# A hybrid attention, RWKV-7 and PEER layer on one core: packed parameters, another order of the first loads, and other queues for three loads of the last stage

## The chip, the cores and the metric

The kernel runs on one NeuronCore of a Trainium2 chip. The metric is the device time of one execution in microseconds. The core has five engines with instruction streams of their own: TensorE (PE, with its weight loads as PEld), VectorE (DVE), ScalarE (ACT), GpSimd (POOL) and SyncE (SP, which here only issues transfers). Each engine takes its instructions in order, and an instruction that waits holds all that stand behind it on that engine. Transfers are issued by SP, ACT or POOL, each into a queue of its own, and are carried by 16 DMA engines that the three queues share.

## The reference, cut to what matters

```python
mod = silu(c) @ ada_w + ada_b                       # shift, scale, gate of two sub-layers
h   = rms_norm(x, norm1_g) * (1 + scale1) + shift1  # x is 1024 tokens x 1024
z   = h @ w_in
x   = x + gate1 * (concat(attention(z), rwkv7(z)) @ w_out)
h2  = rms_norm(x, norm2_g) * (1 + scale2) + shift2
x   = x + gate2 * peer_ffn(h2)

def peer_ffn(h):   # 16384 experts of one neuron each, 8 heads x 16 of them for each token
    # product keys choose the experts e_idx and their gates
    act = gelu(einsum('cd,ced->ce', h, expert_u[e_idx]))
    return einsum('ce,ced->cd', gate * act, expert_v[e_idx])
```

## The kernel before

The program is recorded step by step through a framework that allots buffers from pools, adds the waits that buffers and data ask for, and fixes one order for each engine. Where several lists of steps run side by side, `merge` and `due` in the source say which step comes at what point; the order that results is on record before the run.

**The front** (lines 105 to 266). Some small parameters (`c`, parts of `ada_b`, `norm1_g`, `mu_prev`, `mu_next`, the two norm gains) are loaded in transposed form, one element for each partition and column, by SP's and ACT's queues (L117 to L129); seven more of the same kind (`colp`, L319) come by POOL's. `tables` builds masks on VectorE. Then SP loads sixteen 512 KB tiles `adw` of `ada_w`, and VectorE adds them up in two accumulators `macc` (L223, L225); a first weight tile of `w_in` (two `wraw`) and eight tiles `xx` of x (512 KB each, L233) follow in SP's queue. ScalarE squares every `xx` into row sums (`jk`, L236), and the rows are scaled. Sixteen small products `mcol` turn `macc` into columns, and `h_step` writes the first operand of the input projection, `hTh` and `hTl` (L261 to L263). The first product that uses it is L314.

**The last stage** (from about 2260 us; lines 1750 to 1872) computes PEER in two ways at once. Three blocks of 128 tokens take their experts by gathers: POOL issues an indirect transfer of 512 KB for rows of `expert_u` (`gu`) or `expert_v` (`gv`) at L1361, and VectorE does the products (L1389, L1397). The other five blocks (640 tokens) go densely over all experts, in 128 tiles of 128 experts: for a tile n, `act_half` gives gelu(u h) as the tile `gl` (128 x 640), `gate` multiplies it on POOL with the gates `gt_` (L1771), ScalarE and VectorE split the product into `ah` and `al` (L1772, L1773), and TensorE multiplies these with the split expert rows `vh` and `vl` (L1791, L1792; products L1812 to L1814). VectorE adds the results to `yac` (L1821).

Of the 128 tiles 65 have their gelu computed early, before this stage, and stored in HBM (`actd`); `gate_load` brings such a tile back (320 KB, L1761). `g_load` brings the gates for four tiles (1.25 MB, L1765). `u_load` brings the 512 KB of a tile whose gelu is still to be computed (L1438), `v_load` brings 256 KB of expert rows (L1785). All four are issued by SP.

The stage runs in 32 groups of four tiles; in a group the stored tiles (two, in most groups) come first. Pools limit what can be ahead: two buffers for `gl` (`NGL`), two for `gt_`, two for `u` (`NU`), four for `vr`, four each for `gu` and `gv`. The loads of a group are put into the program by

```python
at(s0, g_load, g)
...
at(s0 + 3 + k - GD, gate_load, n)
at(s0 + 3 + k, gate, n)
```

Of the kernel before, what the change touches and what calls it, by code (L numbers as in the profile page):

```python
# [20 lines left out]
D = 1024  # L21
NB = 8
# [56 lines left out]
def body(tc, nc, I, out, dbg=None):  # L79
# [3 lines left out]
    with root:  # L83
# [30 lines left out]


        scol = ct([128, NK], "scol")
        nc.sync.dma_start(scol, I["c"][0].rearrange("(o p) -> p o", p=128))  # L117
        bcol = ct([128, 16], "bcol")
        nc.scalar.dma_start(bcol, ada_b[0:2048].rearrange("(j p) -> p j", p=128))
        g1col = ct([128, NK], "g1col")  # L120
        nc.scalar.dma_start(g1col, I["norm1_g"][0].rearrange("(j p) -> p j", p=128))
        mup = ct([128, 14], "mup")
        nc.scalar.dma_start(mup, I["mu_prev"][0].rearrange("(j p) -> p j", p=128))
        mun = ct([128, 14], "mun")
        nc.scalar.dma_start(mun, I["mu_next"][0].rearrange("(j p) -> p j", p=128))
        gqk = ct([128, 2], "gqk")
        for i, nm in enumerate(("q_norm_g", "k_norm_g")):
            for h in range(2):
                nc.scalar.dma_start(gqk[64 * h:64 * h + 64, i:i + 1], I[nm][0].rearrange("(p o) -> p o", o=1))  # L129
        nc.scalar.activation(scol, scol, AF.Silu)  # L130
        nc.vector.tensor_scalar(gqk[:, 0:1], gqk[:, 0:1], HD ** -0.5, None, op0=ALU.mult)
# [96 lines left out]
        xt = []  # L228
        ssq = small("ssq", [128, NB])
        rstd = small("rstd", [128, NB])  # L230
        for tb in range(NB):
            xx = slot("xx")
            nc.sync.dma_start(xx, x[tb * 128:(tb + 1) * 128, :])  # L233
            xt.append(xx)
            jk = slot("jk")
            nc.scalar.activation(jk, xx, AF.Square, accum_out=ssq[:, tb:tb + 1])  # L236
            if tb % 4 == 3:
                r_ = rstd[:, tb - 3:tb + 1]
                nc.vector.tensor_scalar(r_, ssq[:, tb - 3:tb + 1], 1.0 / D, 1e-6, op0=ALU.mult, op1=ALU.add)
                rsqrt(r_, r_, [128, 4], "r1")  # L240
                for b in range(tb - 3, tb + 1):
                    if b < 4:
                        nc.vector.tensor_scalar(xt[b], xt[b], rstd[:, b:b + 1], None, op0=ALU.mult)
                    else:
                        nc.scalar.activation(xt[b], xt[b], AF.Copy, scale=rstd[:, b:b + 1])
        mcol = bank("mcol", "po")
# [71 lines left out]

        def colp(name, ap, n):  # L319
            t_ = fc([128, n], name)  # L320
            nc.gpsimd.dma_start(t_, ap.rearrange("(j p) -> p j", p=128))
            return t_

        w0 = [colp(f"w0{d}", I["w_decay0"][0][d], 4) for d in range(2)]
        a0 = [colp(f"a0{d}", I["a_gate0"][0][d], 4) for d in range(2)]
        kkc = colp("kkc", I["k_k"][0], 4)
        kac = colp("kac", I["k_a"][0], 4)
        rkc = colp("rkc", I["r_k"][0].rearrange("h e -> (h e)"), 4)
        ka1 = fc([128, 4], "ka1")
# [1097 lines left out]

        uts, ats = {}, {}
        early = [n for n in range(NT) if (n + 1) * NEARLY // NT > n * NEARLY // NT]
# [397 lines left out]
        def finish_half(tb, hf, y_):  # L1827
# [73 lines left out]
```

## Time and profile before

| | |
|---|---|
| three runs | 3858.38, 3872.6, 3874.69 us; median 3872.6 |
| profiled execution | 3867.33 us, its span 3865.2 us |
| busy share of the span | PE 85%, PEld 75%, DVE 78%, ACT 34%, POOL 45% |
| mean granted TensorE clock | 0.932 of full speed |
| moved by DMA | 862.66 MB, mean 223 GB/s |
| first `hTh` (operand of the input projection) begun | 51.41 us |

The span runs from the first to the last instruction of one execution. A busy share is an average over stages with different limits. The idle time that a view puts beside an instruction stands before it, with the event that ended it. The granted clock is given as a share of 2.4 GHz; 0.5 is 1.2 GHz.

### The profile page before, as it was taken

What the parts mean: (1) busy time and instruction counts of PE and PEld (TensorE: products, weight loads), DVE (VectorE), ACT (ScalarE), POOL (GpSimd) and SP (SyncE); (2) the same over time, 40 slices, a digit from 0 to 9 for tenths busy, and PEclk for the clock granted to TensorE, in tenths of its full rate; (3) what the DMA queues carried; (4) which work ended last, traced back from release to release, by engine and by line L of the source; (5) the groups of instructions that cost most, each with busy time, mean ns of one, the idle gap of its engine ahead of it and who ended that gap; (6) DMA issues with size and microseconds to landing.
All of it is one profiled execution on the core that took longest, in us unless ns stands there. A gap on an engine that the chain in (4) does not pass through costs nothing. (4 is left out here: it accounts for less than half of the span.)

```text
span 3865.2 us, 59635 instructions
## 1 busy us (share of the span) xinstructions
PE 3298.5 (85%) x21937; PEld 2906.7 (75%) x21937; DVE 3004.1 (78%) x5970; ACT 1317.4 (34%) x2710; POOL 1754.6 (45%) x1346
## 2 busy tenths in 40 slices
PE   4968899899697988878878878888889889899998
PEld 4747887677586987877777877777777777777787
DVE  6785556767747799999998977777777878778776
ACT  3234334455212322222377873222222222222221
POOL 2032211222334455466754527555555565655541
PEclk9988999999798988999998999999999999999999
DMA  6434444433464357566798988777777877777774
GB/s 200 177 124 138 140 102 111 113 95 82 124 203 176 115 164 238 173 211 214 270 329 275 342 286 330 285 284 285 289 289 290 301 289 290 291 289 290 295 271 160
DMA packets 493451, 862.66 MB, mean 223 GB/s; under 512 B 149348, under 2 KB 290404, under 8 KB 489064
## 3 DMA queue, kind: packets, MB, share of 16 engines
q1 hardware_dynamic: 372840, 447.20, 35.6%
q0 software_dynamic: 113280, 411.63, 29.0%
q8 instruction: 173, 2.83, 0.3%
q10 hardware_dynamic: 7040, 0.03, 0.1%
q14 instruction: 118, 0.97, 0.1%
HBM read 741.91 MB, written 116.80 MB: 222 GB/s over the span
## 5 line engine op out<-in xcount | busy, mean ns | idle before, releaser
L316 PE MATMUL pact<-dTh,uTl 128*128 128x320 f32 x2048 | 646.2, 317 | 53.9 <-DVE uTl L1449 53.7
L314 PE MATMUL pact<-dTh,uTh 128*128 128x320 f32 x2048 | 648.4, 317 | 24.6 <-ACT uTh L1448 14.3
L315 PE MATMUL pact<-dTl,uTh 128*128 128x320 f32 x2048 | 644.1, 315 | 0.0
L1361 POOL DMA_INDIRECT gu<-in_peer_u_dram,ei x384 | 532.2, 1386 | 221.9 <-DVE gu L1389 135.2
L1389 DVE SCALAR_TENSOR_TENSOR gu<-gu,ghr 128x1024 f32<-128x1024 f32 x384 | 510.1, 1329 | 154.9 <-DMA gu<-in_peer_u_dram,ei 148.3
L1812 PE MATMUL py<-vh,ah 128*128 128x512 f32 x1280 | 522.1, 408 | 98.8 <-DVE yac L1821 58.2
L1813 PE MATMUL py<-vl,ah 128*128 128x512 f32 x1280 | 525.2, 410 | 65.4 <-DVE vl L1792 65.0
L1361 POOL DMA_INDIRECT gv<-in_peer_v_dram,ei x384 | 499.2, 1300 | 158.5 <-issue 89.0
L1397 DVE SCALAR_TENSOR_TENSOR gacc<-gv,gact,gacc 128x1024 f32<-128x1024 f32 x381 | 526.5, 1382 | 54.1 <-DMA gv<-in_peer_v_dram,ei 51.1
L1814 PE MATMUL py<-vh,al 128*128 128x512 f32 x1280 | 517.8, 405 | 2.8 <-DVE al L1773 2.8
L316 PEld LDWEIGHTS pact<-dTh,uTl 128*128 128x128 f32 x2048 | 393.7, 193 | 61.2 <-DVE uTl L1449 61.2
L314 PEld LDWEIGHTS pact<-dTh,uTh 128*128 128x128 f32 x2048 | 395.0, 193 | 30.7 <-ACT uTh L1448 15.8
L315 PEld LDWEIGHTS pact<-dTl,uTh 128*128 128x128 f32 x2048 | 394.1, 192 | 2.5
L1812 PEld LDWEIGHTS py<-vh,ah 128*128 128x128 f32 x1280 | 252.3, 197 | 160.3 <-ACT gl L1460 37.5
L1813 PEld LDWEIGHTS py<-vl,ah 128*128 128x128 f32 x1280 | 252.4, 197 | 139.7 <-DVE vl L1792 88.9
L1814 PEld LDWEIGHTS py<-vh,al 128*128 128x128 f32 x1280 | 252.5, 197 | 56.7 <-DVE al L1773 3.3
L1791 ACT ACTIVATE vh<-vr 128x512 fp32r<-128x512 f32 x256 | 155.9, 625 | 395.8 <-PE py L1814 377.3
L1772 ACT ACTIVATE ah<-gl 128x640 fp32r<-128x640 f32 x128 | 91.2, 735 | 461.2 <-POOL gl L1771 323.5
L1705 DVE TENSOR_TENSOR o<-io,tT 128x1024 f32<-128x1024 f32 x160 | 187.0, 1217 | 34.2 <-ACT tT L161 24.8
L1718 PE MATMUL pgb<-o,o 128*128 128x128 f32 x1280 | 178.4, 295 | 39.0 <-ACT o L1708 29.6
L1448 ACT ACTIVATE uTh<-u 128x1024 fp32r<-128x1024 f32 x128 | 135.1, 1056 | 215.6 <-PE pact L315 174.3
L1773 DVE TENSOR_TENSOR al<-gl,ah 128x640 fp32r<-128x640 f32 x128 | 104.0, 832 | 132.7 <-ACT ah L1772 132.5
(1438 smaller groups left out, 7130.2 us busy)
## 6 DMA issues: line engine op xcount, KB each, us to landing
u<-in_peer_ut_dram SPq DMA_DIRECT2D x128, 512.0 KB
vr<-in_peer_v_dram SPq DMA_DIRECT2D x256, 256.0 KB
Gd<-st SPq DMA_DIRECT2D x160, 256.0 KB
actd<-gl SPq DMA_DIRECT2D x65, 320.0 KB
gl<-actd SPq DMA_DIRECT2D x65, 320.0 KB
awt<-in_ada_w_dram SPq DMA_DIRECT2D x32, 512.0 KB
wraw<-in_peer_w_query_dram SPq DMA_DIRECT2D x32, 512.0 KB
wraw<-in_w_in_dram SPq DMA_DIRECT2D x26, 512.0 KB
```

The costliest lines, as they stand in the source:

```text
L314: nc.tensor.matmul(ps, lh, rh, start=(i == 0), stop=False)
L315: nc.tensor.matmul(ps, lh, rl, start=False, stop=False)
L316: nc.tensor.matmul(ps, ll, rh, start=False, stop=(i == n - 1))
L1361: g_ = nc.gpsimd.indirect_dma_start(out=r_, out_offset=None, in_=src, in_offset=bass.IndirectOffsetOnAxis(ap=eid[tb][:, j:j + 1], axis=0))
L1389: nc.vector.scalar_tensor_tensor(u, u, 1.0, hr, op0=ALU.mult, op1=ALU.mult, accum_out=act[:, q:q + 1])
L1397: nc.vector.scalar_tensor_tensor(acc, v, pact[:, q:q + 1], acc, op0=ALU.mult, op1=ALU.add)
L1705: nc.vector.tensor_tensor(o_, io128[:, None, :].to_broadcast([128, 8, 128]), tT[:, i, t0:t0 + 8, None].to_broadcast([128, 8, 128]), ALU.is ...
L1718: nc.tensor.matmul(pg[:, q * 128:(q + 1) * 128], o1[:, 4 * x_ + q], o2[:, 4 * x_ + q], start=True, stop=True)
L1791: nc.scalar.activation(vh, vts[i], AF.Copy)
L1812: nc.tensor.matmul(ys[hf][b], ah[:, ts], vh, start=(n == tiles[0]), stop=False)
L1813: nc.tensor.matmul(ys[hf][b], ah[:, ts], vl, start=False, stop=False)
L1814: nc.tensor.matmul(ys[hf][b], al[:, ts], vh, start=False, stop=(n == tiles[-1]))
```

## The change

The small parameters are packed on the host side of the program into one array of 128 rows with 90 columns, which one transfer of SP loads; the fourteen small transfers of ACT's and POOL's queues, and that of `c`, are gone. The first four tiles of x are loaded, squared and scaled ahead of `ada_w`; the other four stay where they were. `ada_w` is loaded and added up half by half (all eight tiles of `macc[0]`, then those of `macc[1]`) and no longer alternately. In the last stage the stored tiles `gl` and the gates `gt_` are loaded by POOL's queue, and the `u` tiles by ACT's.

```diff
+        pk = ct([128, 90], "pk")
+        nc.sync.dma_start(pk, I["pk"])
...
+        ccol, bcol, g1col, mup, mun, gqk_ = (cols(n) for n in (NK, 16, NK, 14, 14, 2))
+        w0, a0 = [cols(4) for _ in range(2)], [cols(4) for _ in range(2)]
+        kkc, kac, rkc = (cols(4) for _ in range(3))
         scol = ct([128, NK], "scol")
-        nc.sync.dma_start(scol, I["c"][0].rearrange("(o p) -> p o", p=128))
-        bcol = ct([128, 16], "bcol")
-        nc.scalar.dma_start(bcol, ada_b[0:2048].rearrange("(j p) -> p j", p=128))
...
-        nc.scalar.activation(scol, scol, AF.Silu)
+        nc.scalar.activation(scol, ccol, AF.Silu)
+        nc.vector.tensor_copy(gqk, gqk_)
...
+        def x_in(tbs):
+            for tb in tbs:
+                xx = slot("xx")
+                nc.sync.dma_start(xx, x[tb * 128:(tb + 1) * 128, :])
...
+        x_in(range(4))
 
         macc = [slot("macc") for _ in range(2)]
-        for k in range(NK):
-            for i in range(2):
+        for i in range(2):
+            for k in range(NK):
...
+        x_in(range(4, NB))
...
-            nc.sync.dma_start(u, Ut[n])
+            (nc.scalar if late[0] else nc.sync).dma_start(u, Ut[n])
...
-                nc.sync.dma_start(ats[n], actd[early.index(n)])
+                nc.gpsimd.dma_start(ats[n], actd[early.index(n)])
...
-            nc.sync.dma_start(gts[q], Gd[q])
+            nc.gpsimd.dma_start(gts[q], Gd[q])
...
+        late[0] = True
```

Three places show what moves. On SP in the front, before (the loads of `ada_w`, the first weights, x):

```order
L1088 DMA gu<-in_g_up_dram 128x128
L221 DMA adw<-in_ada_w_dram 128x1024 x16
L180 DMA wraw<-in_w_in_dram 128x4x256 x2
L233 DMA xx<-in_x_dram 128x1024 x8
L180 DMA wraw<-in_w_in_dram 128x4x256 x2
```

and now:

```order
L1083 DMA gu<-in_g_up_dram 128x128
L223 DMA xx<-in_x_dram 128x1024 x4
L243 DMA adw<-in_ada_w_dram 128x1024 x16
L181 DMA wraw<-in_w_in_dram 128x4x256 x2
L223 DMA xx<-in_x_dram 128x1024 x4
L181 DMA wraw<-in_w_in_dram 128x4x256 x2
```

Four of the eight x tiles have moved ahead of the sixteen `adw`.

On POOL in the last stage, between two groups, before (`gu` and `gv` are gathers; `gl_31084` is the first stored tile of the new group, `gl_30959` the last tile of the group before):

```order
L1361 DMA gu_31038<-in_peer_u_dram,ei2_11948 128x1024
L1361 DMA gv_31040<-in_peer_v_dram,ei2_11948 128x1024
L1771 TENSOR_TENSOR gl_31084<-gl_31084,gt__31055 128x640
L1771 TENSOR_TENSOR gl_30959<-gl_30959,gt__30672 128x640
L1361 DMA gu_31078<-in_peer_u_dram,ei2_11948 128x1024
```

and the same place now, up to the load of the group's second stored tile, `gl_31089`:

```order
L1356 DMA gu_31014<-in_peer_u_dram,ei2_11924 128x1024
L1356 DMA gv_31016<-in_peer_v_dram,ei2_11924 128x1024
L1756 DMA gl_31060<-actd_11940 128x640
L1766 TENSOR_TENSOR gl_31060<-gl_31060,gt__31031 128x640
L1766 TENSOR_TENSOR gl_30935<-gl_30935,gt__30648 128x640
L1356 DMA gu_31054<-in_peer_u_dram,ei2_11924 128x1024
L1356 DMA gv_31056<-in_peer_v_dram,ei2_11924 128x1024
L1356 DMA gu_31083<-in_peer_u_dram,ei2_11924 128x1024
L1356 DMA gv_31085<-in_peer_v_dram,ei2_11924 128x1024
L1756 DMA gl_31089<-actd_11940 128x640
```

The load of a group's first stored tile stands right before the product that needs it, with no gather between; that of the second has four gathers between it and its use. In six of the later groups the load of `gt_` stands right before the first one too.

On ACT in the last stage a row of `u` now stands among the conversions (`uTh` and `vh` are the high parts of u and v, `gl` the gelu, `ah` the high part of the gated tile):

```order
L1443 ACTIVATE uTh_32560<-u_32376 128x1024
L1455 ACTIVATE gl_32286<-pact_32313 128x320
L1767 ACTIVATE ah_32409<-gl_32286 128x640
L1786 ACTIVATE vh_32443<-vr_32344 128x512
L1433 DMA u_32756<-in_peer_ut_dram 128x1024
L1786 ACTIVATE vh_32533<-vr_32382 128x512
```

Before, the same stretch of ACT has no transfer in it. The new tile takes the buffer of `u_32376`, which VectorE reads last (`uTl`, the low part).

## Rows read from the trace of the kernel before

**Rows 1.** Stretch of the last stage: length, busy us by engine, clock, DMA share, GB/s

```profile
2260.00:3865.00 1605.00, 1417.96 (x7046) 1221.26 (x7044) 1243.41 (x1600) 387.52 (x685) 869.38 (x643) 0.96 0.77 282
```

**Rows 2.** Waits from 2300 us on: who, for whom, us in total, times, longest

```profile
POOL gl L1771 <- DMA gl<-actd: 249.8, 21, 18.1
...
PE py L1813 <- DVE vl L1792: 65.0, 46, 5.2
PE py L1812 <- DVE yac L1821: 58.2, 21, 4.5
...
DVE gu L1389 <- DMA gu<-in_peer_u_dram,ei: 143.8, 51, 5.4
DVE al L1773 <- ACT ah L1772: 132.5, 31, 11.9
...
SPq L1438 <- DVE uTl L1449: 138.9, 29, 8.0
```

**Rows 3.** Timeline of POOL over three groups: start, us, instruction, idle time before it

```profile
3312.38 1.88 POOL L1771 TENSOR_TENSOR gl<-gl,gt__30286 128x640 f32<-128x640 f32 x1 [14.42 <-issue]
...
3346.59 1.03 POOL L1361 DMA_INDIRECT gv<-in_peer_v_dram,ei  x1 [0.30 <-issue]
3360.14 2.24 POOL L1771 TENSOR_TENSOR gl<-gl,gt__30672 128x640 f32<-128x640 f32 x1 [12.53 <-DMA gl<-actd]
...
3365.14 0.98 POOL L1361 DMA_INDIRECT gu<-in_peer_u_dram,ei  x1
...
3391.56 0.95 POOL L1361 DMA_INDIRECT gv<-in_peer_v_dram,ei  x1 [0.30 <-issue]
...
3410.65 1.57 POOL L1771 TENSOR_TENSOR gl<-gl,gt__31055 128x640 f32<-128x640 f32 x1 [18.14 <-DMA gl<-actd]
```

**Rows 4.** Timeline of SP's queue in the first of these waits

```profile
3346.82 9.20 SPq L1785 DMA_DIRECT2D vr<-in_peer_v_dram  x3
3356.12 0.38 SPq L1761 DMA_DIRECT2D gl<-actd  x1
```

**Rows 5.** The chain of work that ended last, in the same stretch: start, us, what

```profile
3356.12 3.87 DMA gl<-actd
...
3366.43 8.62 DMA gv<-in_peer_v_dram,ei
```

**Rows 6.** Timeline of VectorE in the same stretch

```profile
3345.38 0.81 DVE L1773 TENSOR_TENSOR al<-gl,ah 128x640 fp32r<-128x640 f32 x1
...
3354.99 0.68 DVE L1792 TENSOR_TENSOR vl<-vr,vh 128x512 fp32r<-128x512 f32 x1
...
3373.12 1.23 DVE L1389 SCALAR_TENSOR_TENSOR gu<-gu,ghr 128x1024 f32<-128x1024 f32 x1 [5.16 <-DMA gu<-in_peer_u_dram,ei]
...
3393.87 0.81 DVE L1773 TENSOR_TENSOR al<-gl,ah 128x640 fp32r<-128x640 f32 x1
```

**Rows 7.** Stretches of 4 us while POOL waits, columns as in rows 1

```profile
3348.00:3352.00 4.00, 4.00 (x14) 3.15 (x13) 4.00 (x5) 0.04 (x1) 0.00 (x0) 0.65 1.03 417
3352.00:3356.00 4.00, 4.00 (x29) 4.00 (x28) 4.00 (x8) 1.03 (x2) 0.00 (x0) 1.00 0.54 209
```

**Rows 8.** A plain transfer that POOL issues, line L1309: ns min, median, max

```profile
L1309 POOL DMA_DIRECT2D x1d<-x x8: 534/534/605, 1194.2 to 1209.3; - x8
```

**Rows 9.** Stretches of the front, columns as in rows 1

```profile
0.00:10.00 10.00, 0.00 (x0) 0.00 (x0) 0.21 (x4) 0.00 (x0) 7.39 (x18) 1.00 0.78 60
...
20.00:30.00 10.00, 0.00 (x0) 0.00 (x0) 10.00 (x11) 0.00 (x0) 0.00 (x0) 1.00 1.02 406
```

**Rows 10.** Timeline of the front: VectorE's first waits and sums, the first `hTh`

```profile
13.32 0.17 DVE L332 TENSOR_TENSOR mu<-mup,mun 128x14 f32<-128x14 f32 x1 [12.22 <-DMA mun<-in_mu_next_dram]
...
21.26 9.65 DVE L225 SCALAR_TENSOR_TENSOR macc<-adw,scol,macc 128x1024 f32<-128x1024 f32 x8
...
40.56 1.06 ACT L236 ACTIVATE jk<-xx 128x1024 f32<-128x1024 f32 x1 [0.42 <-DMA xx<-in_x_dram]
...
51.41 0.78 ACT L261 ACTIVATE hTh<-pt,sb,sg 128x512 fp32r<-128x512 f32 x1 [0.19 <-PE pt L257]
```

More of the change, by code (lines that the diff above doesn't have):

```diff
@@ L113, in body, with cols @@
         w_in = I["w_in"][0]
-        scol = ct([128, NK], "scol")
-        nc.sync.dma_start(scol, I["c"][0].rearrange("(o p) -> p o", p=128))
-        bcol = ct([128, 16], "bcol")
-        nc.scalar.dma_start(bcol, ada_b[0:2048].rearrange("(j p) -> p j", p=128))
[L120 to L125, printed above, removed]
+        pk = ct([128, 90], "pk")
+        nc.sync.dma_start(pk, I["pk"])
+        po_ = [0]
+        def cols(n):
+            po_[0] += n
+            return pk[:, po_[0] - n:po_[0]]
+        ccol, bcol, g1col, mup, mun, gqk_ = (cols(n) for n in (NK, 16, NK, 14, 14, 2))
+        w0, a0 = [cols(4) for _ in range(2)], [cols(4) for _ in range(2)]
+        kkc, kac, rkc = (cols(4) for _ in range(3))
+        scol = ct([128, NK], "scol")
         gqk = ct([128, 2], "gqk")
-        for i, nm in enumerate(("q_norm_g", "k_norm_g")):
-            for h in range(2):
-                nc.scalar.dma_start(gqk[64 * h:64 * h + 64, i:i + 1], I[nm][0].rearrange("(p o) -> p o", o=1))
-        nc.scalar.activation(scol, scol, AF.Silu)
+        nc.scalar.activation(scol, ccol, AF.Silu)
+        nc.vector.tensor_copy(gqk, gqk_)
         nc.vector.tensor_scalar(gqk[:, 0:1], gqk[:, 0:1], HD ** -0.5, None, op0=ALU.mult)
@@ L215, in body @@
         tables()
+        xt = []
+        ssq = small("ssq", [128, NB])
+        rstd = small("rstd", [128, NB])
+        def x_in(tbs):
+            for tb in tbs:
+                xx = slot("xx")
+                nc.sync.dma_start(xx, x[tb * 128:(tb + 1) * 128, :])
+                xt.append(xx)
+                jk = slot("jk")
+                nc.scalar.activation(jk, xx, AF.Square, accum_out=ssq[:, tb:tb + 1])
+                if tb % 4 == 3:
+                    r_ = rstd[:, tb - 3:tb + 1]
+                    nc.vector.tensor_scalar(r_, ssq[:, tb - 3:tb + 1], 1.0 / D, 1e-6, op0=ALU.mult, op1=ALU.add)
+                    rsqrt(r_, r_, [128, 4], "r1")
+                    for b in range(tb - 3, tb + 1):
+                        if b < 4:
+                            nc.vector.tensor_scalar(xt[b], xt[b], rstd[:, b:b + 1], None, op0=ALU.mult)
+                        else:
+                            nc.scalar.activation(xt[b], xt[b], AF.Copy, scale=rstd[:, b:b + 1])
+        x_in(range(4))
         macc = [slot("macc") for _ in range(2)]
-        for k in range(NK):
-            for i in range(2):
+        for i in range(2):
+            for k in range(NK):
                 a = slot("adw")
@@ L227, in body @@
         WT = {GO[0]: load_w(w_in, GO[0] * 256, nc.gpsimd)}
[L228 to L245, printed above, removed]
+        x_in(range(4, NB))
         mcol = bank("mcol", "po")
@@ L316, in mm3 @@
                 nc.tensor.matmul(ps, ll, rh, start=False, stop=(i == n - 1))
[L319 to L328, printed above, removed]
         ka1 = fc([128, 4], "ka1")
@@ L1425, in gathers @@
                 next(gt, None)
-        uts, ats = {}, {}
+        uts, ats, late = {}, {}, [False]
         early = [n for n in range(NT) if (n + 1) * NEARLY // NT > n * NEARLY // NT]
@@ L1872, in body @@
         pe.close()
-_INS = ['x', 'c', 'ada_w', 'ada_b', 'norm1_g', 'w_in', 'mu_prev', 'mu_next', 'q_norm_g', 'k_norm_g', 'w_decay0',
-        'w_decay_up', 'a_gate0', 'a_gate_up', 'g_up', 'k_k', 'k_a', 'r_k', 'lnx_g', 'lnx_b', 'w_out', 'norm2_g',
+_INS = ['x', 'ada_w', 'ada_b', 'w_in',
+        'w_decay_up', 'a_gate_up', 'g_up', 'lnx_g', 'lnx_b', 'w_out', 'norm2_g',
         'peer_w_query', 'peer_sub_keys1', 'peer_sub_keys2', 'peer_u', 'peer_v']
@@ L1890 @@
         args[name] = nc.dram_tensor(f"in_{name}_dram", a.shape, mybir.dt.from_np(a.dtype), kind="ExternalInput").ap()
+    P = lambda n: _np.asarray(inputs[n])[0].reshape(-1)
+    a = [P("c"), P("ada_b")[:2048], P("norm1_g"), P("mu_prev"), P("mu_next")] + [P(n) for n in ("q_norm_g", "k_norm_g") for _ in range(2)]
+    a = _np.concatenate(a + [P(n) for n in ("w_decay0", "a_gate0", "k_k", "k_a", "r_k")])
+    a = _np.ascontiguousarray(a.reshape(-1, 128).T)
+    arrays["in_pk_dram"] = a
+    args["pk"] = nc.dram_tensor("in_pk_dram", a.shape, mybir.dt.from_np(a.dtype), kind="ExternalInput").ap()
     a = inputs["peer_u"]
```

## The prediction

> **What bounds the kernel now.** I read the table by stretch first, then the waits, then the timelines of POOL, SP and VectorE about one wait, and last the chain. In the last stage the reader is to see that PE is busy for 1417.96 of 1605 us and no other engine for more than 1243 [rows 1]. That is 1417.96 / 32 = 44.3 us in each of the 32 groups. A group lasts (3410.65 - 3312.38) / 2 = 49.1 us [rows 3]. So PE is near its limit but not at it: 4.8 us of a group are at stake, 4.8 x 31 = 149 us in all (the first group starts with the stage and has no such wait).
>
> What holds the other 4.8 us is a loop. POOL stands idle once in a group, for 14.42, 12.53 and 18.14 us, before the product of the first stored tile [rows 3]; the waits put most such stretches down to the load of `gl` [rows 2]. In the stretch at 3347 us, POOL is done with its gathers at 3346.59 + 1.03 = 3347.62 [rows 3], and the buffer for `gl` is free when VectorE's `al` ends, at 3346.19 [rows 6]. Yet SP issues the load only at 3356.12, because the `vr` loads stand ahead of it [rows 4] and each needs a buffer that a `vl` of VectorE must free; the last such `vl` began at 3354.99 [rows 6]. The load lands 3.87 us later [rows 5], at 3359.99. Only then can POOL issue gathers, and one issued there lands after 8.62 us [rows 5], so VectorE stands idle for 5.16 us [rows 6]. Its `vl` and `yac` come late in turn, and PE waits for them, 65.0 and 58.2 us in total [rows 2]. The late `vl` delays SP again.
>
> **The last stage, part by part.** The 65 stored `gl` and 32 `gt_` leave SP, and the `u` loads too. Nothing is added to what is transferred.
>
> *The first stored tile of a group.* The load is now POOL's own instruction, right before the product, with no gather between, so POOL must still wait for its whole landing. Two kinds of group alternate. In the first (3347 us) the issue moves from 3356.12 to 3347.7. In POOL's queue it stands behind gathers that are still under way. Between 3348 and 3356 the DMA engines moved 4 x 0.417 + 4 x 0.209 = 2.5 MB [rows 7], none of it `gl`; I take all of it to be ahead, and with the tile's own 0.33 MB that is 2.8 MB, at 0.417 MB/us 6.8 us. With 0.83 us for the issue (0.53 [rows 8] and the 0.30 that POOL stands before each issue [rows 3]) it lands at 3355.3 instead of 3360.0: 4.7 us gained. In the second kind POOL is free at 3392.51 [rows 3] but `al` ends at 3394.68 [rows 6], so the issue waits 2.2 us, in which the queue carries 0.9 MB; the rest takes 4.6 us, and the tile lands at about 3399.8 instead of 3410.5: 10.7 us. The mean is 7.7 us.
>
> *What it charges.* POOL issues (65 + 32) / 32 = 3.03 more transfers in a group, 0.83 us each: 2.5 us. The second stored tile has four gathers between load and use, 4 x (0.98 + 0.30) = 5.1 us [rows 3], and needs 6.8: POOL waits 1.7 us more, and the gathers behind this product wait with it. Net of a group: 7.7 - 2.5 - 1.7 = 3.5 us. In six of the later groups the 1.25 MB of `gt_` stand right ahead of `gl`: 1.25 / 0.417 = 3.0 us more, net 0.5. The sum is 25 x 3.5 + 6 x 0.5 = 90 us. The ends: the most is PE's limit, 149 us; the least, if the tile lands no earlier than before and POOL pays all the charges, is 31 x (2.5 + 1.7) = 130 us lost. I take 90, since the stretch at 3352 has the DMA engines busy only 0.54 [rows 7], and the wait there was for an issue and not for bandwidth.
>
> That a product on POOL comes 3.5 us earlier shortens the group by as much only because the gathers stand behind it in order, and VectorE's work on them in order again. What is late next is PE itself, then the `ah` of ScalarE that `al` waits for (132.5 us [rows 2]).
>
> *The price of a POOL issue.* The trace has eight plain transfers from POOL, 534 to 605 ns each, taken while the queue is quiet [rows 8]; an issue in the midst of gathers is nearest to the gathers' own 0.95 to 1.03 us [rows 3]. With 1.33 in place of 0.83 us, the group loses 1.5 us more, and the sum is 90 - 31 x 1.5 = 43 us; I take the lower price, since the load has no index to follow. The Trainium skill, in "DMA: Bandwidth & Descriptors", section "SWDGE vs HWDGE vs iDMA", says that a transfer issued by GpSimd has its descriptors computed by software, and one by SyncE or ScalarE by hardware, with a faster setup. The trace shows POOL's own time only, not what passes before the first byte; that speaks for the higher price and against this change.
>
> *The `u` loads on ACT.* A `u` load waits until VectorE has written `uTl`. SP stood 138.9 us in 29 such waits, 8.0 at most [rows 2]. Now ACT stands there, and behind it are conversions `vh`. What hides this is VectorE: the `vl` that PE needs beside each `vh` is behind the same `uTl` on VectorE, so PE would be waiting anyway; I cost it at nothing. If that cover is gone, it is up to 138.9 us over the stage, 4.3 in a group, which is within the lower end above. For SP it is a gain of the same kind, since its `vr` loads no longer stand behind `u`, `gt_` and `gl`: `vr` can come as soon as a buffer is free. I give it no price of its own (0 to the 1.3 us that remain to the limit of 4.8).
>
> **The front.** In the first 10 us the DMA engines are 0.78 busy for 60 GB/s [rows 9]: the small transposed loads hold them. VectorE waits 12.22 us for `mun` [rows 10]. Sixteen `adw`, two `wraw` and eight `xx` are 26 x 0.524 = 13.6 MB, at 406 GB/s [rows 9] 33.6 us. With one packed load ahead they start at about 4 us (the nearest landing is 3.87 us [rows 5]) and end at 38. VectorE's 16 sums take 16 x 9.65 / 8 = 19.3 us [rows 10] and stay beside them. Behind the last `xx` are now four squares instead of eight, 1.06 us each [rows 10], most of them beside the loads: the first `hTh` begins at about 40 instead of 51.41 us [rows 10], 11 gained. The ends are 4 (only the four squares) and 13 (all that remains of the loads' late start).
>
> The sum is 3867.3 - 90 - 11 = 3766 us, against the profiled execution's own time. The median of the runs shown is 5.3 us above that one. I give 3768.
>
> **The rivals.** *PE's limit is reached.* Once SP has fewer loads, `vr` runs ahead as well, and all 149 us come back; with 11 of the front, 3867.3 - 160 = 3707. For it: PE's waits are few, 123 us by these two rows [rows 2]. Against it: POOL still waits some 7 us in each group.
>
> *Only the front counts.* POOL frees itself earlier, but the tile lands as late as before, because the DMA engines are the limit: charges fall within the wait, and only 11 us remain, 3856. For it: the engines are full at 3348 [rows 7] and 0.77 busy over the stage [rows 1]. Against it: 0.54 at 3352, and a landing 3.87 us after the issue [rows 5, 7]. The Trainium skill says of this, in "DMA: Bandwidth & Descriptors", section "Issuing engines are not separate DMA queues", that transfers from all three issuers run on the same 16 engines, and that several issuers save only the time of issuing, usually small. By that rule the time would be 3856; in this trace the issue itself is held for 9 us by what stands before it, which the rule does not count.
>
> *POOL's queue makes it slower.* The load now stands behind gathers in one queue, and POOL, which waits for it, issues no others. The tile may land later than the mean of about 15 us after POOL is free that it does now; with the charges of 4.2 it decides at 15 - 4.2 = 10.8 us from POOL's being free. At 14 us a group is 3.2 us longer: 3867.3 + 31 x 3.2 - 11 = 3955. For it: a gather takes 8.62 us to land [rows 5], more than my 6.8. Against it: the engines move 2.5 MB in 8 us even when half idle [rows 7].
>
> **How the numbers follow.** My forecast has 0.62, PE's limit 0.12, only the front 0.14, POOL's queue 0.12. A measurement of this kernel tells about 0.5%, 19 us, from no change. So faster by more is 0.74, within 0.14, slower 0.12. The forecast's own range goes from 3720 (front 13, a net of 4.3 in all groups) to 3830 (the higher price of an issue). The range for 8 in 10 takes in the limit of PE and the front alone: 3695 to 3864; it leaves out the slower case and the tails.
>
> **What would show it.** Right: POOL's idle stretch before the first stored tile falls from about 15 to about 7 us; the load of `gl` is issued as soon as `al` ends and lands 5 to 8 us later; VectorE's waits for gathers shrink; a group lasts about 46 us; the first `hTh` is at about 40 us; ACT's waits for `uTl` are long without PE's waits for `vh` growing. Wrong: a wait of 11 us or more between load and product on POOL; plain issues on POOL of 1 us or more; PE waiting for `vh` more than for `vl`; or a group of 49 us with POOL idle for less, which would mean that POOL's wait did not set the group.

## The result and the profile after

The changed kernel takes 3817.83 us (median of 4 runs, 3805.94 to 3824.67), the kernel before 3870.55 us (median of 4) on the same chip. The ratio is 0.9866, with an interval of 0.9832 to 0.9899: 1.34% or about 52 us faster. The forecast was 3768 us, a gain of twice that; its range (3695 to 3864) holds the time, and its direction is right. The profiled execution took 3816.53 us and its span is 3814.8 us.

In the changed kernel's line numbers L1771 is L1766 (the product), L1361 is L1356 (the gathers), L1792 is L1787 (`vl`), L1449 is L1444 (`uTl`) and L1438 is L1433 (the load of `u`). The stretch of the last stage, columns as in [rows 1]:

```profile
2250.00:3815.00 1565.00, 1411.65 (x7148) 1226.19 (x7148) 1313.53 (x1615) 405.04 (x723) 991.27 (x744) 0.96 0.81 293
```

Against [rows 1] the stage is 1565 instead of 1605 us, and PE's busy time is within 7 us of it. VectorE, with the same kind and number of instructions to within 15, is busy for 70 us longer, and POOL for 122 us, of which 97 issues at 0.60 us explain 58. The rest is the same work at a higher price; a likely reason comes at the end. The waits from 2300 us on (who, line, for whom: us in total, times, longest):

```profile
POOL gl L1766 <- DMA gl<-actd: 247.6, 42, 14.7
...
ACT vh L1786 <- DVE uTl L1444: 121.8, 33, 8.1
...
PE py L1808 <- DVE vl L1787: 106.0, 47, 5.9
...
POOL gl L1766 <- ACT gl L1455: 93.7, 26, 19.4
DVE gu L1384 <- DMA gu<-in_peer_u_dram,ei: 88.7, 57, 4.3
...
PE py L1807 <- ACT vh L1786: 2.5, 2, 1.4
```

The last of these rows was, before:

```profile
PE py L1812 <- ACT vh L1791: 12.7, 2, 12.4
```

Beside [rows 2], VectorE's wait for gathers fell from 143.8 to 88.7, and `al`'s wait for `ah` from 132.5 to 24.2. POOL's wait for `gl`, 247.6 against 249.8, seems not to have changed, but the rows count by releaser: before, many stretches in front of the first stored tile stand under other names ("issue" in [rows 3]). Counted by place, from the second group on, POOL stood there for 437 us in all before and for 235 us now, in the mean of the sixth to the thirtieth group 14.74 and 8.41 us. PE's wait for `vl`, which was to stay, rose from 65.0 to 106.0, and that for `vh` fell. POOL over a group, as in [rows 3]:

```profile
3272.53 0.59 POOL L1756 DMA_DIRECT2D gl<-actd  x1
3280.32 2.52 POOL L1766 TENSOR_TENSOR gl<-gl,gt__30262 128x640 f32<-128x640 f32 x1 [7.20 <-DMA gl<-actd]
...
3328.76 2.42 POOL L1766 TENSOR_TENSOR gl<-gl,gt__30648 128x640 f32<-128x640 f32 x1 [6.49 <-DMA gl<-actd]
```

The idle stretch before the first stored tile is 7.20 and 6.49 us, where it was 12.5 to 18.1 [rows 3], and an issue takes 0.59 us. In the chain the load's landing is itself a link now:

```profile
3272.53 7.71 DMA gl<-actd
```

7.71 us against the 3.87 of [rows 5]: the tile is issued earlier and lands more slowly, as the prediction had it. A group, from its first product on POOL to that of the next (mean of 25, the sixth to the thirtieth), lasts 47.03 us; before, it was 48.69. The waits and groups below are means of the same 25.

### The profile page after: what moved, and what is told of

Read it like the earlier page. It is cut to its first block, busy times and chain, and to the rows that moved or that the text cites. A ratio compares the mean times of both kernels' runs of the same rounds, so it can differ in the third digit from the quotient of the medians.

```text
span 3814.8 us, 59453 instructions
## 1 busy us (share of the span) xinstructions
PE 3279.8 (86%) x21937; PEld 2898.6 (76%) x21937; DVE 3068.9 (80%) x5971; ACT 1322.7 (35%) x2710; POOL 1858.5 (49%) x1436
## 4 chain that ended last, share of the span: by engine, by line
PE 29%; DVE 25%; issue 16%; POOL 14%; DMA 13%; ACT 2%; SPq 1%; POOLq 0%; DVEq 0%; ACTq 0%
POOL gv L1356 6%; POOL gu L1356 5%; DVE gu L1384 4%; DVE gacc L1392 3%; PE psz L319 3%; PE psz L320 3%; PE psz L321 3%; DMA gl<-actd 3%; DMA gv<-in_peer_v_dram,ei 3%; DMA gu<-in_peer_u_dram,ei 3%; DVE ef L1625 2%; POOL gl L1766 2%; DVE uTl L1444 1%; DVE o L1700 1%; PE pact L321 1%
## 5 line engine op out<-in xcount | busy, mean ns | idle before, releaser
L1356 POOL DMA_INDIRECT gu<-in_peer_u_dram,ei x384 | 531.0, 1383 | 205.7 <-DVE gu L1384 122.1
L1392 DVE SCALAR_TENSOR_TENSOR gacc<-gv,gact,gacc 128x1024 f32<-128x1024 f32 x381 | 543.2, 1426 | 88.0 <-DMA gv<-in_peer_v_dram,ei 80.8
L1808 PE MATMUL py<-vl,ah 128*128 128x512 f32 x1280 | 520.3, 406 | 106.2 <-DVE vl L1787 106.0
L1384 DVE SCALAR_TENSOR_TENSOR gu<-gu,ghr 128x1024 f32<-128x1024 f32 x384 | 528.0, 1376 | 102.8 <-DMA gu<-in_peer_u_dram,ei 92.8
L1356 POOL DMA_INDIRECT gv<-in_peer_v_dram,ei x384 | 526.8, 1372 | 153.9 <-issue 106.7
L1807 PE MATMUL py<-vh,ah 128*128 128x512 f32 x1280 | 512.9, 401 | 22.7 <-ACT ah L1767 20.0
L1787 DVE TENSOR_TENSOR vl<-vr,vh 128x512 fp32r<-128x512 f32 x256 | 199.5, 781 | 30.5 <-ACT vh L1786 30.5
L1713 PEld LDWEIGHTS pgb<-o,o 128*128 128x128 f32 x1280 | 170.2, 203 | 45.0 <-ACT o L1703 44.5
```

Of the source, the lines that this page charges most:

```text
L1356: g_ = nc.gpsimd.indirect_dma_start(out=r_, out_offset=None, in_=src, in_offset=bass.IndirectOffsetOnAxis(ap=eid[tb][:, j:j + 1], axis=0))
L1384: nc.vector.scalar_tensor_tensor(u, u, 1.0, hr, op0=ALU.mult, op1=ALU.mult, accum_out=act[:, q:q + 1])
L1392: nc.vector.scalar_tensor_tensor(acc, v, pact[:, q:q + 1], acc, op0=ALU.mult, op1=ALU.add)
L1713: nc.tensor.matmul(pg[:, q * 128:(q + 1) * 128], o1[:, 4 * x_ + q], o2[:, 4 * x_ + q], start=True, stop=True)
L1787: nc.vector.tensor_tensor(vl, vts[i], vh, ALU.subtract)
L1807: nc.tensor.matmul(ys[hf][b], ah[:, ts], vh, start=(n == tiles[0]), stop=False)
```

## The experiments

Ratios are to the kernel before on the same chip, with 95% intervals. The runs lie on three chips, so they are compared with each other by these ratios. The first four take the change apart.

### Only the front (e1_front_only)

```diff
-            (nc.scalar if late[0] else nc.sync).dma_start(u, Ut[n])
+            nc.sync.dma_start(u, Ut[n])
...
-                nc.gpsimd.dma_start(ats[n], actd[early.index(n)])
+                nc.sync.dma_start(ats[n], actd[early.index(n)])
...
-            nc.gpsimd.dma_start(gts[q], Gd[q])
+            nc.sync.dma_start(gts[q], Gd[q])
```

> The changed kernel with the last stage's three loads back in SP's queue: the front alone. Theory A (the front's gain is mostly lost again before the last stage): the first hTh begins at 46.5 us, 5 us earlier than before; the second u tile of the stage at 1200 us waits for a POOL store as in the changed kernel (its buffer lies where the last row block of h lay), SP issues it some 41 us late, and that costs 9 to 10 us; so the time is 0 to 6 us above the kernel before. Rival B (the delay at 1214 us came from the last stage's queues or by chance): no such delay, and 4 to 11 us below the kernel before. Groups of the last stage 48.5 us, as before, by both.

Measured: 3861.9 us, ratio 0.9999 [0.9986, 1.0012]. The front is worth nothing, to within 5 us, and not 11 us.

### Only the queues (e2_queues_only)

The kernel before, with the three queue edits of the change and nothing else:

```diff
-            nc.sync.dma_start(u, Ut[n])
+            (nc.scalar if late[0] else nc.sync).dma_start(u, Ut[n])
...
-                nc.sync.dma_start(ats[n], actd[early.index(n)])
+                nc.gpsimd.dma_start(ats[n], actd[early.index(n)])
...
-            nc.sync.dma_start(gts[q], Gd[q])
+            nc.gpsimd.dma_start(gts[q], Gd[q])
```

> The kernel before with the last stage's three loads moved as in the change, and the front untouched. Theory A: no delay at 1214 us, groups of 46.8 us, and all the gain of the change and a little more: 50 to 60 us below the kernel before. Rival B: the front gives its share too, so this one gains only 40 to 47 us.

Measured: 3815.0 us, 0.9867 [0.9852, 0.9882]. That is the whole effect of the change.

### Only `u` on ScalarE's queue (e3_u_on_act)

The changed kernel with `gl` and `gt_` back on SP:

```diff
-                nc.gpsimd.dma_start(ats[n], actd[early.index(n)])
+                nc.sync.dma_start(ats[n], actd[early.index(n)])
...
-            nc.gpsimd.dma_start(gts[q], Gd[q])
+            nc.sync.dma_start(gts[q], Gd[q])
```

> The changed kernel with gl and gt_ back in SP's queue; only the u tiles go by ACT's. Theory A (POOL's wait for the stored tile sets the group): POOL still waits some 12 to 18 us before the first stored tile, groups of 47.5 to 48.5 us, the time within 20 us of the kernel before. Rival C (the gain comes from SP, whose vr loads no longer stand behind u loads that wait for uTl): groups of about 47, 35 to 55 us below the kernel before.

Measured: 3988.81 us, 1.0324 [1.031, 1.0338]. This is the part that the prediction priced at nothing. VectorE's timeline about one wait for a gather, in this kernel:

```profile
3380.81 1.56 DVE L1768 TENSOR_TENSOR al<-gl,ah 128x640 fp32r<-128x640 f32 x2 [4.94 <-ACT ah L1767]
3389.07 1.22 DVE L1384 SCALAR_TENSOR_TENSOR gu<-gu,ghr 128x1024 f32<-128x1024 f32 x1 [6.70 <-DMA gu<-in_peer_u_dram,ei]
...
3390.22 0.69 DVE L1787 TENSOR_TENSOR vl<-vr,vh 128x512 fp32r<-128x512 f32 x1
```

The same place in the kernel with only the front:

```profile
3311.88 1.56 DVE L1768 TENSOR_TENSOR al<-gl,ah 128x640 fp32r<-128x640 f32 x2 [3.75 <-ACT ah L1767]
3313.36 0.69 DVE L1787 TENSOR_TENSOR vl<-vr,vh 128x512 fp32r<-128x512 f32 x1
3318.78 1.23 DVE L1384 SCALAR_TENSOR_TENSOR gu<-gu,ghr 128x1024 f32<-128x1024 f32 x1 [4.74 <-DMA gu<-in_peer_u_dram,ei]
```

With `u` on ScalarE's queue the program has `vl` and the `gu` product the other way round, so `vl` stands behind a wait of 6.70 us for a gather it doesn't need. PE pays for it (the waits of this kernel):

```profile
PE py L1808 <- DVE vl L1787: 225.2, 31, 9.7
```

With only the front this row has 70.8 us. VectorE waits 205.9 us for `gu` here, against 134.8, so what stands behind such a wait comes later still. That the order is all of the 124 us is not shown: in this kernel POOL also waits 8.37 us in a group for the gelu of the first live tile (one whose gelu is computed in this stage), where e1 has 0.46, and PE's granted clock in the stage is 0.91 against 0.96 (PE is busy for 9 us more).

### Only `gl` on POOL (e4_gl_on_pool)

```diff
-            (nc.scalar if late[0] else nc.sync).dma_start(u, Ut[n])
+            nc.sync.dma_start(u, Ut[n])
...
-            nc.gpsimd.dma_start(gts[q], Gd[q])
+            nc.sync.dma_start(gts[q], Gd[q])
```

> The changed kernel with gt_ and u back in SP's queue; only the stored tiles gl go by POOL's. Theory A: nearly the whole gain of the last stage, or more, since POOL issues 32 loads less and the 1.25 MB of gt_ no longer stand ahead of gl in its queue: groups of 46 to 47 us, POOL's wait before the first stored tile 6 to 8 us, 45 to 75 us below the kernel before. Rival C (SP's queue is what counts): SP still holds its vr loads behind u, the groups stay at 48 us, and the time is within 20 us of the kernel before.

Measured: 3808.19 us, 0.9851 [0.9832, 0.987], about 57 us. The wait before the first stored tile fell from a mean of 14.92 us (e1) to 7.80, so the term of 7.7 us is right (7.1). But a group fell only from 48.52 to 47.11 us, 1.4 net. The forecast for `gl` alone was 7.7 - 1.7 - 1.7 = 4.3 (3.5 with the issue of `gt_`). That SP, freed of `gl`, could bring `vr` sooner is not what pays: ScalarE waits 8.6 us for `vr` over the stage here and 8.2 us in e1. POOL in one group of this kernel:

```profile
3270.73 1.75 POOL L1766 TENSOR_TENSOR gl<-gl,gt__30262 128x640 f32<-128x640 f32 x1 [7.76 <-DMA gl<-actd]
3275.67 2.29 POOL L1766 TENSOR_TENSOR gl<-gl,gt__29879 128x640 f32<-128x640 f32 x1 [3.19 <-ACT gl L1455]
...
3292.66 1.94 POOL L1766 TENSOR_TENSOR gl<-gl,gt__30262 128x640 f32<-128x640 f32 x1 [2.44 <-DMA gl<-actd]
```

The next two products wait now: the last tile of the group before (second row) 2.0 us in the mean where e1 has 0.0, the second stored tile (third row) 2.3 where e1 has 0.1. That is 4.2 us more, of which 1.7 was forecast, for the second stored tile alone. The products take 1.98 us each instead of 1.76.

### The `u` loads back on SP (e5_u_back_on_sp)

```diff
-            (nc.scalar if late[0] else nc.sync).dma_start(u, Ut[n])
+            nc.sync.dma_start(u, Ut[n])
```

> The changed kernel with only the u tiles back in SP's queue (gl and gt_ stay with POOL). On VectorE this puts one vl of each group ahead of the product that waits for a gather, where the changed kernel has it behind. Theory A (that vl, for which PE waits, is what the u tiles on ACT cost): PE's waits for vl fall below the 106 us of the changed kernel, and the time is 55 to 75 us below the kernel before, at or below the run with gl alone on POOL. Rival C (SP's relief is worth something beside POOL's): it is slower than the changed kernel, 20 to 45 us below the kernel before.

Measured: 3792.43 us, 0.9814 [0.9798, 0.983], below the change's 0.9866 and e2's 0.9867, whose interval ends at 0.9852. So `u` on ScalarE's queue costs 0.52%, some 20 us. It differs from the changed kernel in that line alone, yet 31 of VectorE's instructions stand at another place, nearly all of them like this (- is the changed kernel, + this one):

```
 L1768 TENSOR_TENSOR al<-gl,ah 128x640 x2
-L1384 SCALAR_TENSOR_TENSOR gu,gact<-gu,ghr 128x1024
-L1787 TENSOR_TENSOR vl<-vr,vh 128x512
+L1787 TENSOR_TENSOR vl<-vr,vh 128x512
+L1384 SCALAR_TENSOR_TENSOR gu,gact<-gu,ghr 128x1024
```

The changed kernel has 28 places of the first kind in the stage, this one has one. One such place on VectorE's timeline, in the changed kernel:

```profile
3334.78 1.55 DVE L1768 TENSOR_TENSOR al<-gl,ah 128x640 fp32r<-128x640 f32 x2
3340.31 1.23 DVE L1384 SCALAR_TENSOR_TENSOR gu<-gu,ghr 128x1024 f32<-128x1024 f32 x1 [3.98 <-DMA gu<-in_peer_u_dram,ei]
...
3341.46 0.69 DVE L1787 TENSOR_TENSOR vl<-vr,vh 128x512 fp32r<-128x512 f32 x1
```

and one in this kernel, where `vl` no longer waits for the gather:

```profile
3320.74 0.68 DVE L1787 TENSOR_TENSOR vl<-vr,vh 128x512 fp32r<-128x512 f32 x1
3324.89 1.23 DVE L1384 SCALAR_TENSOR_TENSOR gu<-gu,ghr 128x1024 f32<-128x1024 f32 x1 [3.47 <-DMA gu<-in_peer_u_dram,ei]
```

### `vl` first again, `u` still on ScalarE's queue (e9_vl_first)

The changed kernel, with a constraint on VectorE's order alone: a `gu` product may not stand ahead of a `vl` that was written earlier.

```diff
+                    if lastv[0] is not None:
+                        tc.add_manual_dep(p_.ins, lastv[0].ins.name,
...
+                lastv[0] = nc.vector.tensor_tensor(vl, vts[i], vh, ALU.subtract)
```

> The changed kernel, u tiles on ACT as in it, with one constraint: on VectorE a product gu that is recorded behind a vl may not be put ahead of it. The pattern al, gu, vl (a vl behind a product that waits for a gather) goes from 28 places to 6. Theory A (what the u tiles on ACT cost is this order on VectorE): PE's waits for vl fall below 100 us, and most of the 20 to 25 us come back, 65 to 78 us below the kernel before. Rival E (ACT itself costs it: its conversions vh stand behind the u load that waits for uTl): no more than 5 us better than the changed kernel, 45 to 58 us below the kernel before.

Measured: 3807.03 us, 0.9828 [0.9806, 0.9851], with 6 places of that kind left. How much of the 20 us comes back is not settled: 15 by the ratios, 7 by the medians (59.6 us below the kernel before, where the changed kernel is 52.7 and e5 73.1 below), 8 by the group, 46.76 us against 47.03. The interval meets that of the changed kernel and that of e5. So the order is likely a part of the cost; that it is most of it is not shown. PE's waits for `vl` are less than half those of the changed kernel:

```profile
ACT ah L1771 <- DVE uTl L1448: 139.3, 15, 10.4
...
PE py L1812 <- DVE vl L1791: 46.1, 50, 6.8
```

But these waits do not go with the time. With `u` on SP's queue, e4 has nearly those of the changed kernel, and e5, which is faster than e9, has more than e9 (the row of e4, then of e5):

```profile
PE py L1808 <- DVE vl L1787: 103.1, 48, 5.4
...
PE py L1808 <- DVE vl L1787: 89.1, 51, 7.7
```

So most of the rise from 65.0 to 106.0 us came with `gl` on POOL and not with `u`; why is open. The constraint also did more than undo the exchange: 102 of VectorE's instructions stand elsewhere than in the changed kernel. What remains to e5 (46.01 us in a group) is open too: ScalarE still stands in its queue for `uTl` (the first row above).

### Only `gt_` on POOL (e12_gt_on_pool)

```diff
-            (nc.scalar if late[0] else nc.sync).dma_start(u, Ut[n])
+            nc.sync.dma_start(u, Ut[n])
...
-                nc.gpsimd.dma_start(ats[n], actd[early.index(n)])
+                nc.sync.dma_start(ats[n], actd[early.index(n)])
```

> The changed front; only gt_ by POOL's queue, gl and u by SP's. Theory A (POOL's wait for gl, in SP's queue, still sets the group; gt_ is worth something only once gl is early): within 12 us of the kernel before. Rival F (the 1.25 MB of gt_, which SP issues just as POOL takes up its gathers again, delay these by themselves, so that moving it pays alone): 20 to 40 us below.

Measured: 3836.87 us, 0.993 [0.9911, 0.9949]: 27 us gained by the part that was booked as a charge. POOL's wait before the first stored tile is unchanged (14.47 us), so it is not that wait. SP, POOL and VectorE in the kernel with only the front:

```profile
3360.38 0.33 SPq L1760 DMA_DIRECT2D gt__31031<-Gd  x1
3360.51 0.98 POOL L1356 DMA_INDIRECT gu<-in_peer_u_dram,ei  x1 [0.16 <-issue]
...
3368.35 1.23 DVE L1384 SCALAR_TENSOR_TENSOR gu<-gu,ghr 128x1024 f32<-128x1024 f32 x1 [5.03 <-DMA gu<-in_peer_u_dram,ei]
```

In SP's order the 1.25 MB of gates start at the moment when POOL, free again, issues its first gathers, and VectorE waits 5.03 us for one. On POOL the load falls in the middle of a group; the same wait in this kernel:

```profile
3339.59 1.23 DVE L1384 SCALAR_TENSOR_TENSOR gu<-gu,ghr 128x1024 f32<-128x1024 f32 x1 [1.30 <-DMA gu<-in_peer_u_dram,ei]
```

Over the stage VectorE's waits for `gu` fall from 134.8 us (e1) to 46.2, and with `gl` on POOL from 125.7 (e4) to 57.3 (e5). That the gates' transfer delays the gathers is read from these rows; no run moves it on SP's queue alone.

### The product put later (e7_product_later_sp, e8_product_later_pool)

If POOL's idle spot alone set the group, a product that stands six gathers later would free the same time without any load on another queue. e7 has all loads on SP, e8 has `gl` on POOL; both hold the first stored tile's product behind the gathers that are written before it:

```diff
-            pace[0] = nc.gpsimd.tensor_tensor(g3, g3, gts[n // TA][:, :, n % TA], ALU.mult)
+            tt_ = nc.gpsimd.tensor_tensor(g3, g3, gts[n // TA][:, :, n % TA], ALU.mult)
+            if n == order[n // GR][0] and lastg[0] is not None:
+                tc.add_manual_dep(tt_.ins, lastg[0].ins.name,
...
```

> No load leaves SP's queue; the front is that of the change. In each group the product of the first stored tile is put six gathers later in POOL's order, so that these gathers no longer wait for it. Theory A (what cost was POOL standing in order before this product, whoever issues the load): POOL's wait of 15 us shrinks to 5 us or less, VectorE's and PE's waits shrink with it, groups of 45 to 47 us, 50 to 120 us below the kernel before. Rival D (PE or VectorE set the group, POOL's wait is slack): groups of 48 us, within 20 us of the kernel before.

> gl by POOL's queue (gt_ and u by SP's), and the product of the first stored tile six gathers behind its load in POOL's order. Theory A: the load's 7 us lie under the gathers, POOL waits no more than 1 to 3 us there, the group comes near PE's 44.3 us: 80 to 140 us below the kernel before. Rival D (with POOL's wait down to 7 us another engine sets the group already): the same time as gl on POOL alone, 50 to 65 us below.

Measured: e7 3862.76 us, 0.9994 [0.998, 1.0009]; e8 3828.16 us, 0.9909 [0.9894, 0.9924], slower than e4. The wait did not go, it moved to the products of the two live tiles, whose gelu is written into the `gl` buffers that come free last. In e7 POOL waits 0.02 us before the first stored tile, but 4.0 and 11.3 us before the live ones (the waits of e7):

```profile
POOL gl L1767 <- ACT gl L1456: 456.2, 58, 18.9
...
ACT gl L1456 <- DVE al L1775: 145.4, 29, 9.7
```

So the loop runs through the `gl` buffers: product, `ah`, `al`, the next load or gelu. That only a tile that comes round it sooner helps is how these two runs are read; no run has more buffers.

### The front mended (e6_front_mended)

Only the front, with the first weights loaded behind x, and the names of two row blocks of h swapped so that the block used last might lie elsewhere:

```diff
-TO = "wr wh wl g2r jk h0 h1 h2 h3 h4 h5 h6 h7"
+TO = "wr wh wl g2r jk h7 h1 h2 h3 h4 h5 h6 h0"
...
-        WT = {GO[0]: load_w(w_in, GO[0] * 256, nc.gpsimd)}
...
+        WT = {GO[0]: load_w(w_in, GO[0] * 256, nc.gpsimd)}
```

> The front alone (all loads of the last stage in SP's queue) with two edits: the last row block of h changes its buffer with the first one, so that the u tile at 1200 us waits for an early store instead of the last, and the first weights of w_in are loaded after x, so that POOL's wl no longer runs beside VectorE's sums macc. Theory A: the delay at 1214 us is gone (9 to 10 us) and the second eight sums take 1.2 us each again, so that the first hTh begins at 41 to 44 us; 8 to 16 us below the kernel before. Rival B: the sums are paced by the loads and not by POOL (hTh at 46 us), or the delay at 1214 us stays; 0 to 5 us below.

Measured: 3865.74 us, 1.0009 [0.9996, 1.0022]: no gain. In the changed kernel the last seven sums over `ada_w` run beside two products of POOL (timeline):

```profile
29.23 13.16 DVE L247 SCALAR_TENSOR_TENSOR macc<-adw,scol,macc 128x1024 f32<-128x1024 f32 x7
...
35.42 5.89 POOL L173 TENSOR_TENSOR wl<-wraw,wh 128x1024 fp32r<-128x1024 f32 x2 [32.91 <-ACT wh L172]
...
42.44 3.57 PE L253 MATMUL mcol<-ones,macc 128*128 128x1 f32 x16 [10.29 <-DVE macc L247]
...
46.53 0.78 ACT L266 ACTIVATE hTh<-pt,sb,sg 128x512 fp32r<-128x512 f32 x1 [4.64 <-DVE rstd L229]
```

and in e6, with these products moved:

```profile
28.95 9.21 DVE L247 SCALAR_TENSOR_TENSOR macc<-adw,scol,macc 128x1024 f32<-128x1024 f32 x7
...
43.62 4.26 ACT L235 ACTIVATE xx<-xx,rstd 128x1024 f32<-128x1024 f32 x4 [1.11 <-DVE rstd L103]
47.80 1.99 ACT L172 ACTIVATE wh<-wraw 128x1024 fp32r<-128x1024 f32 x2
...
49.69 2.76 ACT L266 ACTIVATE hTh<-pt,sb,sg 128x512 fp32r<-128x512 f32 x4
```

The sums are 4 us shorter, as expected, but ScalarE now has the scaling of x and `wh` ahead of the first `hTh`, which begins later still. The swap of names did not free the `u` load at 1200 us, which is described with the next run: the distance measured there is that of the changed kernel.

### The last row block of h elsewhere (e10_h_buffer_moved)

e5, with four unused row blocks allotted ahead of the last one, so that the early `u` tiles no longer share its place:

```diff
-TO = "wr wh wl g2r jk h0 h1 h2 h3 h4 h5 h6 h7"
+TO = "wr wh wl g2r jk h0 h1 h2 h3 h4 h5 h6 dm0 dm1 dm2 dm3 h7"
...
+                    if b == NB - 1:
+                        for i in range(4):
+                            nc.gpsimd.memset(tl[f"dm{i}"][:, 0:1], 0.0)
```

> gl and gt_ by POOL's queue, u by SP's (as in the run with u back on SP), and four unused row blocks are allotted before the last block of h, so that its buffer no longer lies under the u tile that SP loads at 1200 us. Theory A (the packed front lost 9 to 10 us there): SP issues this u tile and the next loads without that wait, the delay against the kernel before at 1214 us is gone, and the time is 80 to 88 us below the kernel before, some 9 us under the run with u back on SP. Rival B (the wait only moves, because hr needs the last stores anyway): within 3 us of that run, 68 to 75 us below.

Measured: 3782.88 us, 0.9783 [0.9764, 0.9802], the fastest of all, 2.2% below the kernel before. What it aims at lies at 1200 us, between the sums of h and the first `wl` of the weights that follow. VectorE there, in the changed kernel:

```profile
1194.01 1.40 DVE L1299 SCALAR_TENSOR_TENSOR h<-x,ss,pT 128x512 f32<-128x512 f32 x2
...
1230.72 1.23 DVE L1532 TENSOR_TENSOR wl<-wraw,wh 128x1024 fp32r<-128x1024 f32 x1 [0.31 <-ACT wh L1531]
```

From the one to the other are 36.7 us; the same distance is 36.7 to 36.9 in e1, e4, e5, e6 and e12, which have the new front, 27.0 in the kernel before, e2 and e11, which have the old one, and 31.3 here. So the new front costs 9.7 us at this place, and the edit takes 5.4 of them away. SP's queue there, in the changed kernel:

```profile
1183.70 41.13 SPq L1433 DMA_DIRECT2D u<-in_peer_ut_dram  x2
...
1226.03 6.26 SPq L1503 DMA_DIRECT2D hr<-h2d  x3
```

in the kernel before:

```profile
1190.52 0.84 SPq L1438 DMA_DIRECT2D u<-in_peer_ut_dram  x2
...
1214.20 15.69 SPq L1508 DMA_DIRECT2D hr<-h2d  x3
```

and here, with POOL's row for the unused blocks:

```profile
1184.57 0.42 SPq L1497 DMA_DIRECT2D sk<-in_peer_sub_keys_dram  x1
1215.99 0.80 SPq L1436 DMA_DIRECT2D u<-in_peer_ut_dram  x2
...
1218.67 9.65 SPq L1506 DMA_DIRECT2D hr<-h2d  x3
...
1215.80 0.20 POOL L1298 MEMSET dm<- 128x1 f32 x4
```

In the changed kernel the second `u` load lies on the place of the last row block of h and waits until that is done with (it waits for three semaphores where it waited for one), and SP stands there for 41 us, with `hr` behind it. Here that wait is gone, but another has come: SP stands 31 us before the first `u` load, until POOL, at 1215.80 us, writes the unused blocks, one of which lies on that load's place. Both `u` loads still start 25 us later than before. That this is what the remaining 4.3 us are is likely, and no run shows it. In time e10 is 0.31% below e5, which is more than 5.4 us and near the intervals' width.

### The old front, `gl` and `gt_` on POOL (e11_old_front)

The kernel before with two of its lines changed:

```diff
-                nc.sync.dma_start(ats[n], actd[early.index(n)])
+                nc.gpsimd.dma_start(ats[n], actd[early.index(n)])
...
-            nc.sync.dma_start(gts[q], Gd[q])
+            nc.gpsimd.dma_start(gts[q], Gd[q])
```

> The kernel before with only gl and gt_ moved to POOL's queue: two lines changed, the front untouched, u in SP's queue. Theory A (the front's net is a loss of about 5 us): 74 to 86 us below the kernel before. Rival B (the front's gain counts): it is slower than the same queues with the packed front, 60 to 68 us below.

Measured: 3786.2 us, 0.9795 [0.9775, 0.9815]. Two lines give more than the whole change, without the loss at 1200 us. By the intervals neither e10 nor e5 is told apart from it, so what the front costs or gives beside these queues stays below 0.5%.

## Why the prediction was half right

**The wait of POOL: right in mechanism and size.** It said 15 us would become about 7, the issue 0.6 us long at the lower price, the landing 5 to 8 us. Measured: 14.92 to 7.80 us (e1 to e4), 14.74 to 8.41 in the change itself, 0.60 us, 7.71 us in the group shown.

**Its net in a group: mis-sized, for `gl` alone 4.3 forecast, 1.4 measured (e4).** The issues of `gl`, 2.03 in a group, cost 1.2 us, where 1.7 was reckoned for them. In place of the 1.7 for the second stored tile two waits grew, by 4.2 in all: 2.2 there and 2.0 before the last tile of the group before. The prediction looked only at the one tile's landing, not at the two buffers through which all products of a group come round (e7, e8). That leaves 7.1 - 1.2 - 4.2 = 1.7. The products' own slowing, some four of them by 0.22 us, was not in the sum at all: 0.9 more, partly under the same waits.

**The gates: the wrong sign.** They were a charge, 0.83 us for an issue in every group and 3.0 us more in six; alone they gain 27 us (e12), and by e12's rows because SP's place for them collided with the gathers that VectorE waits for. The prediction asked what POOL pays for the load and not whom it had disturbed. With this, `gl` and `gt_` together gain 72 us (e5) where 90 were forecast.

**`u` on ScalarE's queue: the step that failed.** "I cost it at nothing", because `vl` would be late behind `uTl` anyway. It costs 20 us here and 124 alone (e3). That cover says why a late `vh` would cost nothing; it does not hold when `vl` itself gets later. The move of one load changed the order in which VectorE's work is written, and `vl` came to stand behind a gather. Taking that back returned 7 to 15 of the 20 us (e9); what the rest is stays open. The sign that the prediction set, ScalarE's waits for `uTl` without PE's waits for `vh` growing, came true (121.8 us, and 12.7 to 2.5), and did not warn, because it looks at `vh`. The rows of the order by engine, which were read for POOL, SP and ScalarE, would have shown it on VectorE.

**The front: 11 forecast, 0 measured (e1).** The loads end at 39 us as reckoned. But the sums were priced at 9.65 / 8 [rows 10] beside nothing, and POOL's products, which the new order put beside them, made seven take 13.16 instead of 9.21 us. The `mcol` products behind the sums, 3.57 us, were left out of the sum. So the first `hTh` is at 46.53 and not at 40. What was left, 4.9 us against [rows 10], is less than the 9.7 us lost at 1200 us, 5.4 of them to a buffer's new place. Between the two, the same instructions wander by more: the sums of h at 1200 us are 7.3 us early in the changed kernel and 0.3 late in e1, with nothing different up to there.

**The sum.** By the ratios: -57 (`gl`), -15 more with `gt_` (alone 27, so part of it is the same time), +20 (`u`), 0 (front): -52. Forecast, term by term: 31 x 4.3 = 133 gained by `gl`, 31 x 0.83 + 6 x 3.0 = 44 lost by `gt_`, 0 by `u`, 11 gained by the front, so 100 (101 in the prediction's rounding). That the time lies within the range is in part luck: the gates missed the other way than the rest. Of the rivals, PE's limit did not come (44.1 us of PE in a group of 47), nor did a slower POOL queue (it decided at 10.8 us; the wait is 7.8 to 8.4). "Only the front counts" was wrong in both halves. The Trainium skill's rule by which that rival came out ("DMA: Bandwidth & Descriptors", "Issuing engines are not separate DMA queues": only issuing time is saved) does not hold as a price here: two lines that change the issuer alone gain 2% (e11), and one alone loses 3.2% (e3), through what stands behind the issue in an engine's order, and with `u` through another order on VectorE.

## What to carry to other kernels

Before a load is moved to another queue, ask what its old place held up or collided with, and read the new order on every engine, not only on the two queues: a scheduler may rearrange the engine that does the waiting. Test the parts of a bundle apart, since here two lines of it are worth more than all of it. A rearranged front can lose far behind what it gained, where a shifted buffer makes an in-order queue wait.

## What of the hardware was not expected

VectorE and GpSimd slow each other. Seven sums of 1024 columns with two operands in SBUF took 13.16 us where 5.89 us of GpSimd products lay beside them and 9.21 where none did (e6). Five of the seven took 1.285 us each, as all seven do in e6; the two beside the products took 3.27 and 3.26, and each ended 1.08 us after a product did (at 39.10 and 42.39 us, the products at 38.02 and 41.31). The two products took 2.60 and 3.33 us, where they take 2.34 each in e6. So the two engines worked nearly one after the other. The Trainium skill says so in "SBUF — State Buffer", section "Who interferes with whom": a VectorE instruction with two inputs in SBUF contends with a GpSimd one that reads SBUF, and one waits for the other. In the last stage `vl` takes 703 ns in the mean before, 781 in the changed kernel and 816 in e4. The same contention is the likely source of VectorE's 70 us more of busy time, which no run here isolates.

TensorE's clock fell early in the new front. The changed kernel by stretches of 4 us, columns as in [rows 1]:

```profile
20.00:24.00 4.00, 2.29 (x11) 1.88 (x9) 3.89 (x4) 0.00 (x0) 0.00 (x0) 1.00 1.03 411
24.00:28.00 4.00, 0.00 (x0) 0.00 (x0) 3.89 (x4) 0.00 (x0) 0.00 (x0) 0.74 1.03 410
28.00:32.00 4.00, 3.42 (x16) 3.42 (x16) 3.89 (x5) 0.00 (x0) 0.00 (x0) 0.50 1.02 401
```

PE did transposes, stood idle from 24 us, and the granted clock went to 0.50, the lower level of 1.2 GHz; it is still there in the stretch from 52 to 56 us, where the kernel before has 1.00. That one falls to 0.50 too, in the stretch from 60 to 64 us. What the earlier fall costs was not tried by itself.
